# FiLM layer on one core: two slabs of 64 rows in place of four of 32, longer runs in the first store, and each projection loaded by two transfers

## The chip, the cores and the metric

The kernel runs on one core of a Trainium2 chip. Times are device microseconds of one execution; a kernel's time is the median of its runs. The profile's span, in the run that was profiled, is shorter than its time by about 1.8 us, so differences can be read in either. "Faster" or "slower" would need 2%; most of what follows is about tenths of a per cent, so the intervals are given.

## The reference

```python
batch, seq, dim, cond_dim = 32, 512, 256, 64
gamma = conditioning @ gamma_proj          # 32 x 256
beta = conditioning @ beta_proj
return (x * (1 + gamma[:, None, :]) + beta[:, None, :]).astype(np.float32)
```

x is 16.78 MB of float32 and the output is as large. The two small products need 0.14 MB: conditioning and the two projections, gamma_proj and beta_proj.

## The kernel before

x is cut into slabs. A slab puts consecutive rows of 1 KB on each of the 128 partitions, so one partition's share of a slab is one contiguous run in HBM (32 rows, 32 KB). All loads are issued on SP's queue, the constants and all stores on ACT's queue.

```python
SLABS = 4; BS = batch // SLABS; REP = P // BS; ROWS = BS * seq // P     # ROWS = 32
x_v = x.flatten_outer_dims().rearrange("(s p r) d -> s p r d", s=SLABS, p=P)
LOADS = {0: [8, 8, 8, 8], 3: [26, 6]}          # rows per load; others: one load of 32
STORES = {0: (32,), 1: (32,), 2: (32,), 3: (16, 32)}
GROUP = 16; ON_DVE = 11
# ...
nc.scalar.dma_start(out=gbproj[0::2, :], in_=gamma_proj)      # rows interleaved over
nc.scalar.dma_start(out=gbproj[1::2, :], in_=beta_proj)       # the 128 partitions
# ... conditioning is transposed and replicated by a matmul with a replicated identity;
# ... per slab a pair of matmuls gives gamma and beta, one row for each partition (PSUM);
# ... ACT copies them to SBUF (gb_s) for GpSimd; VectorE reads them from PSUM
for s in range(SLABS):
    for r0 in range(0, ROWS, GROUP):
        # VectorE: 11 of 16 rows, (gamma + 1) * x, then + beta;  GpSimd: the other 5
        # ...
        if s == 0 and r0 + GROUP == ROWS:      # "the hold": no store before the last
            nc.scalar.copy(out=held,           # but one load has landed
                           in_=slabs[-1][:, LOADS[SLABS - 1][0] - 1, 0:1])
        for e0, e1 in zip((0,) + STORES[s], STORES[s]):
            if r0 < e1 <= r0 + GROUP:
                nc.scalar.dma_start(out=o_v[s, :, e0:e1, :], in_=xs[:, e0:e1, :])
```

The hold: the copy of one element makes ACT wait for the 26-row load, so that no store begins among the loads before it, and the last 6-row load covers the time that the first store needs to get going (before: issued at 41.08, first packet at 41.96; the packets of the 6-row load end at 42.29).

Of the kernel before, what the change touches and what calls it, by code (L numbers as in the profile page):

```python
# [2 lines left out]

# [5 lines left out]


@with_exitstack
def kernel(
    ctx: ExitStack,
    tc: tile.TileContext,
    x: bass.AP,
    conditioning: bass.AP,
    gamma_proj: bass.AP,
    beta_proj: bass.AP,
    out: bass.AP,  # L20
):
    nc = tc.nc
    f32 = mybir.dt.float32
    ALU = mybir.AluOpType

    batch, seq, dim = x.shape
    cond_dim = conditioning.shape[1]
    P = 128
    SLABS = 4
    BS = batch // SLABS  # L30
    REP = P // BS
    ROWS = BS * seq // P
    assert SLABS * BS == batch and REP * BS == P and ROWS * REP == seq

    x_v = x.flatten_outer_dims().rearrange("(s p r) d -> s p r d", s=SLABS, p=P)
    o_v = out.flatten_outer_dims().rearrange("(s p r) d -> s p r d", s=SLABS, p=P)

    LOADS = {0: [8, 8, 8, 8], 3: [26, 6]}
    STORES = {0: (32,), 1: (32,), 2: (32,), 3: (16, 32)}
    GROUP = 16  # L40
    ON_DVE = 11

    consts = ctx.enter_context(tc.tile_pool(name="consts", bufs=1))
    xpool = ctx.enter_context(tc.tile_pool(name="xpool", bufs=1))
    psum = ctx.enter_context(tc.tile_pool(name="psum", bufs=1, space=bass.MemoryType.PSUM))


    cond_s = consts.tile([batch, cond_dim], f32)
    nc.scalar.dma_start(out=cond_s, in_=conditioning)  # L49

    gbproj = consts.tile([2 * cond_dim, dim], f32)
    nc.scalar.dma_start(out=gbproj[0::2, :], in_=gamma_proj)  # L52
    nc.scalar.dma_start(out=gbproj[1::2, :], in_=beta_proj)

    slabs = []
    for s in range(SLABS):
        xs = xpool.tile([P, ROWS, dim], f32, name=f"xs{s}")
        slabs.append(xs)
        r = 0
        for n in LOADS.get(s, [ROWS]):  # L60
            nc.sync.dma_start(out=xs[:, r : r + n, :], in_=x_v[s, :, r : r + n, :])
            r += n
        assert r == ROWS


    ident = consts.tile([batch, batch], f32)
    make_identity(nc, ident)
    rident = consts.tile([batch, batch * REP], f32)
    nc.vector.tensor_copy(  # L69
        out=rident.rearrange("p (b g) -> p b g", g=REP),  # L70
        in_=ident.to_broadcast([batch, batch, REP]),
    )


    cond_T = []
    for h in range(2):
        wide = consts.tile([batch, cond_dim, 2], f32, name=f"wide{h}")
        nc.vector.memset(wide, 0.0)  # L78
        nc.vector.tensor_copy(out=wide[:, :, h], in_=cond_s)  # L79
        t_p = psum.tile([2 * cond_dim, batch * REP], f32, name=f"cond_T_p{h}")  # L80
        nc.tensor.matmul(t_p, lhsT=wide.rearrange("b k h -> b (k h)"), rhs=rident,  # L81
                         start=True, stop=True)
        t_s = consts.tile([2 * cond_dim, batch * REP], f32, name=f"cond_T{h}")
        nc.vector.tensor_copy(out=t_s, in_=t_p)  # L84
        cond_T.append(t_s)

    gb_p, gb_s = [], []
    for s in range(SLABS):
        p_t = psum.tile([P, 2 * dim], f32, name=f"gb_p{s}")
        for h in range(2):  # L90
            nc.tensor.matmul(p_t[:, h * dim : (h + 1) * dim],  # L91
                             lhsT=cond_T[h][:, s * P : (s + 1) * P], rhs=gbproj,
                             start=True, stop=True)
        s_t = consts.tile([P, 2 * dim], f32, name=f"gb_s{s}")
        nc.scalar.activation(out=s_t[:, :dim], in_=p_t[:, :dim],  # L95
                             func=mybir.ActivationFunctionType.Identity,
                             bias=1.0, scale=1.0)
        nc.scalar.copy(out=s_t[:, dim:], in_=p_t[:, dim:])  # L98
        gb_p.append(p_t)
        gb_s.append(s_t)  # L100

    def rows(t, n):
        return bass.AP(tensor=t.tensor, offset=t.offset, ap=[t.ap[0], [0, n], t.ap[1]])

    held = consts.tile([P, 1], f32)
    with tc.manual_schedule():
        for s in range(SLABS):
            xs = slabs[s]
            g_p, b_p = gb_p[s][:, :dim], gb_p[s][:, dim:]
            g_s, b_s = gb_s[s][:, :dim], gb_s[s][:, dim:]  # L110
            for r0 in range(0, ROWS, GROUP):
                v = xs[:, r0 : r0 + ON_DVE, :]
                w = xs[:, r0 + ON_DVE : r0 + GROUP, :]
                nv, nw = ON_DVE, GROUP - ON_DVE
                nc.vector.scalar_tensor_tensor(out=v, in0=rows(g_p, nv), scalar=1.0, in1=v,  # L115
                                               op0=ALU.add, op1=ALU.mult)
                nc.gpsimd.tensor_tensor(out=w, in0=w, in1=rows(g_s, nw), op=ALU.mult)  # L117
                nc.vector.tensor_add(out=v, in0=v, in1=rows(b_p, nv))  # L118
                nc.gpsimd.tensor_tensor(out=w, in0=w, in1=rows(b_s, nw), op=ALU.add)  # L119
                if s == 0 and r0 + GROUP == ROWS:  # L120

                    nc.scalar.copy(out=held, in_=slabs[-1][:, LOADS[SLABS - 1][0] - 1, 0:1])  # L122

                for e0, e1 in zip((0,) + STORES[s], STORES[s]):
                    if r0 < e1 <= r0 + GROUP:
                        nc.scalar.dma_start(out=o_v[s, :, e0:e1, :], in_=xs[:, e0:e1, :])
            assert STORES[s][-1] == ROWS


# [1 line left out]
_INS = ['x', 'conditioning', 'gamma_proj', 'beta_proj']  # L131
_OUTS = [((32, 512, 256), 'float32')]


# [23 lines left out]
```

## Time and profile before

| | before |
|---|---|
| time | 84.08 us (84.04 to 84.08, 3 runs) |
| span | 82.4 us |
| DMA queues | 48.3% + 48.1% of 16 engines' span |
| VectorE, GpSimd busy | 62%, 56% |
| first packet begins, last packet ends | 1.73, 81.28 us |

The page's lines are shown in the prediction below. They are read like this: in the rows of digits each digit is a fortieth of the span, 9 meaning busy for 90% or more. A row of the table of stretches gives the stretch, then busy time (and number of instructions) of PE, weight loads, VectorE, ACT and GpSimd, then the TensorE clock, the DMA share and the GB/s moved. Bytes are credited by packet, so a stretch's GB/s wobbles with large packets, and the DMA share can pass 1.

### The profile page before, as it was taken

To read this page: it belongs to the slowest core of one execution; us is meant where nothing else is said; L and a number is where in the kernel's file an instruction comes from. 1 tells how busy PE (TensorE), PEld (TensorE's weight loads), DVE (VectorE), ACT (ScalarE), POOL (GpSimd) and SP (SyncE) were. 2 spreads that over 40 slices of the span, in tenths; PEclk is the share of its full clock that TensorE was granted. 3 is DMA by queue.
4 is the path that set the end of the run, shared out by engine and by line. 5 is a ranking of instruction groups with operands and counts; after the bars stand their busy time and mean duration, and the time that the engine had idled before them with its cause. 6 is when DMAs were issued, how large, how long until landed. Compare 5 with 4: busy or idle time off the path is not lost.

```text
span 82.4 us, 180 instructions
## 1 busy us (share of the span) xinstructions
PE 9.4 (11%) x20; PEld 5.5 (7%) x20; DVE 51.1 (62%) x23; ACT 4.1 (5%) x10; POOL 46.4 (56%) x22
## 2 busy tenths in 40 slices
PE   0069799200000000000000000000000000000000
PEld 0041478000000000000000000000000000000000
DVE  1023307999999999999999999999990000000000
ACT  0600017400000000000000000000000000000000
POOL 2000008999999999999999999999600000000000
PEclk9999999998555555555555555555555555555555
DMA  3899999979979998999797996996995999789992
GB/s 52 322 417 426 429 425 541 461 318 493 493 334 445 509 397 370 439 465 452 301 564 318 509 493 270 509 493 270 509 509 254 509 509 429 334 382 493 397 397 111
DMA packets 2080, 33.69 MB, mean 409 GB/s; under 512 B 288, under 2 KB 416, under 8 KB 544
## 3 DMA queue, kind: packets, MB, share of 16 engines
q1 hardware_dynamic: 1152, 16.78, 48.3%
q10 hardware_dynamic: 928, 16.92, 48.1%
HBM read 16.92 MB, written 16.78 MB: 409 GB/s over the span
## 4 chain that ended last, share of the span: by engine, by line
DVE 43%; issue 17%; DMA 9%; PE 4%; ACTq 1%; ACT 1%
DVE xs L115 30%; DVE xs L118 13%; DMA gbproj<-in_beta_proj_dram 9%; PE gb_p L91 4%; ACTq L52 1%; ACTq L49 0%; ACT gb_s L95 0%; ACT gb_s L98 0%
## 5 line engine op out<-in xcount | busy, mean ns | idle before, releaser
L117 POOL TENSOR_TENSOR xs<-xs,gb_s 128x1280 f32<-128x1280 f32 x8 | 23.1, 2889 | 11.5 <-ACT gb_s L95 11.5
L115 DVE SCALAR_TENSOR_TENSOR xs<-gb_p,xs 128x2816 f32<-128x2816 f32 x8 | 24.7, 3083 | 3.5 <-ACT gb_s L98 3.5
L118 DVE TENSOR_TENSOR xs<-xs,gb_p 128x2816 f32<-128x2816 f32 x8 | 24.7, 3087 | 0.3
L119 POOL TENSOR_TENSOR xs<-xs,gb_s 128x1280 f32<-128x1280 f32 x8 | 23.1, 2886 | 0.6
L91 PE MATMUL gb_p<-gbproj,cond_T 128*128 128x256 f32 x16 | 5.7, 530 | 0.6 <-DMA gbproj<-in_beta_proj_dram 0.6
L91 PEld LDWEIGHTS gb_p<-gbproj,cond_T 128*128 128x128 f32 x16 | 4.4, 280 | 3.1 <-issue 2.1
L81 PE MATMUL cond_T_p<-rident,wide 32*128 32x512 f32 x4 | 3.8, 1096 | 4.8 <-DVE rident L69 4.8
L84 DVE COPY cond_T<-cond_T_p 128x512 f32<-128x512 f32 x2 | 1.4, 692 | 3.2 <-PE cond_T_p L81 3.2
L79 DVE COPY wide<-cond_s 32x64 f32<-32x64 f32 x2 | 0.3, 182 | 3.0 <-DMA cond_s<-in_conditioning_dram 3.0
L95 ACT ACTIVATE gb_s<-gb_p 128x256 f32<-128x256 f32 x4 | 1.5, 384 | 9.3 <-PE gb_p L91 9.3
L81 PEld LDWEIGHTS cond_T_p<-rident,wide 32*128 32x128 f32 x4 | 1.2, 318 | 5.9 <-DVE rident L69 4.8
L98 ACT COPY gb_s<-gb_p 128x256 f32<-128x256 f32 x4 | 1.5, 367 | 0.0
L122 ACT COPY held<-xs 128x1 f32<-128x1 f32 x1 | 0.2, 192 | 25.3 <-DMA xs<-in_x_dram 25.3
L95 ACT ACT_TABLE_LOAD x1 | 1.3, 1283 | 2.4 <-issue 2.4
L78 DVE MEMSET wide<- 32x128 f32 x2 | 0.3, 165 | 0.8 <-PEq L142 0.8
L69 DVE COPY rident<-ident 32x512 f32<-32x512 f32 x1 | 0.4, 406 | 0.0
masks.py:197 POOL MEMSET ident<- 32x32 f32 x1 | 0.1, 114 | 0.3 <-POOLq L142 0.3
masks.py:199 POOL TENSOR_SCALAR_AFFINE_SELECT ident<-ident 32x32 f32<-32x32 f32 x1 | 0.2, 202 | 0.1
L142 POOL MEMSET const-float32-0.0<- 128x1 f32 x1 | 0.1, 104 | 0.2 <-issue 0.2
L142 POOL MEMSET const-bfloat16-1.0<- 128x1 bf16 x1 | 0.1, 107 | 0.0
L142 POOL MEMSET const-uint8-127<- 128x1 uint8 x1 | 0.1, 107 | 0.0
L142 POOL MEMSET const-float32-1.0<- 128x1 f32 x1 | 0.1, 104 | 0.0
## 6 DMA issues: line engine op xcount, KB each, us to landing
out_dram<-xs ACTq DMA_DIRECT2D x3, 4096.0 KB, 20.5
xs<-in_x_dram SPq DMA_DIRECT2D x2, 4096.0 KB, 24.6
xs<-in_x_dram SPq DMA_DIRECT2D x4, 1024.0 KB, 8.3
out_dram<-xs ACTq DMA_DIRECT2D x2, 2048.0 KB, 20.3
xs<-in_x_dram SPq DMA_DIRECT2D x1, 3328.0 KB, 35.2
xs<-in_x_dram SPq DMA_DIRECT2D x1, 768.0 KB, 35.1
gbproj<-in_gamma_proj_dram ACTq DMA_DIRECT2D x1, 64.0 KB, 6.4
gbproj<-in_beta_proj_dram ACTq DMA_DIRECT2D x1, 64.0 KB, 7.3
```

The lines of the kernel that those rows point to most:

```text
L52: nc.scalar.dma_start(out=gbproj[0::2, :], in_=gamma_proj)
L69: nc.vector.tensor_copy(out=rident.rearrange("p (b g) -> p b g", g=REP), in_=ident.to_broadcast([batch, batch, REP]),)
L81: nc.tensor.matmul(t_p, lhsT=wide.rearrange("b k h -> b (k h)"), rhs=rident, start=True, stop=True)
L84: nc.vector.tensor_copy(out=t_s, in_=t_p)
L91: nc.tensor.matmul(p_t[:, h * dim : (h + 1) * dim], lhsT=cond_T[h][:, s * P : (s + 1) * P], rhs=gbproj, start=True, stop=True)
L95: nc.scalar.activation(out=s_t[:, :dim], in_=p_t[:, :dim], func=mybir.ActivationFunctionType.Identity, bias=1.0, scale=1.0)
L98: nc.scalar.copy(out=s_t[:, dim:], in_=p_t[:, dim:])
L115: nc.vector.scalar_tensor_tensor(out=v, in0=rows(g_p, nv), scalar=1.0, in1=v, op0=ALU.add, op1=ALU.mult)
L117: nc.gpsimd.tensor_tensor(out=w, in0=w, in1=rows(g_s, nw), op=ALU.mult)
L118: nc.vector.tensor_add(out=v, in0=v, in1=rows(b_p, nv))
L119: nc.gpsimd.tensor_tensor(out=w, in0=w, in1=rows(b_s, nw), op=ALU.add)
L142: nc = _bacc.Bacc("TRN2", target_bir_lowering=False, num_devices=1)
```

## The change

The intent is fewer and larger pieces: half the slabs, so half of the small matmul and copy work in front, and the first slab's result written in runs of 64 KB. Each projection is loaded by two transfers of 32 rows.

```diff
-    SLABS = 4
+    SLABS = 2
...
-    LOADS = {0: [8, 8, 8, 8], 3: [26, 6]}
-    STORES = {0: (32,), 1: (32,), 2: (32,), 3: (16, 32)}
+    LOADS = {0: [8, 8, 8, 8, 32], 1: [32, 26, 6]}
+    STORES = {0: (64,), 1: (32, 64)}
...
-    nc.scalar.dma_start(out=gbproj[0::2, :], in_=gamma_proj)
-    nc.scalar.dma_start(out=gbproj[1::2, :], in_=beta_proj)
+    half = cond_dim // 2
+    for h, proj in enumerate((gamma_proj, beta_proj)):
+        for c0 in (0, half):
+            nc.scalar.dma_start(out=gbproj[2 * c0 + h : 2 * (c0 + half) : 2, :],
+                                in_=proj[c0 : c0 + half, :])
...
-                    nc.scalar.copy(out=held, in_=slabs[-1][:, LOADS[SLABS - 1][0] - 1, 0:1])
+                    nc.scalar.copy(out=held, in_=slabs[-1][:, ROWS - LOADS[SLABS - 1][-1] - 1, 0:1])
```

## The prediction

> **What bounds the kernel now.** I read the page from the top: the slices, then the DMA queues, then the table of stretches, and only then the chain of waits, because that chain ends at a compute instruction and would mislead here.
>
> ```profile
> span 82.4 us, 180 instructions
> PE 9.4 (11%) x20; PEld 5.5 (7%) x20; DVE 51.1 (62%) x23; ACT 4.1 (5%) x10; POOL 46.4 (56%) x22
> ...
> DVE  1023307999999999999999999999990000000000
> ...
> DMA  3899999979979998999797996996995999789992
> ...
> q1 hardware_dynamic: 1152, 16.78, 48.3%
> q10 hardware_dynamic: 928, 16.92, 48.1%
> ```
>
> The reader is to see that no compute engine is busy in the last ten of forty slices, while the DMA row is near full from the second slice to the last but one. The two DMA queues (q1 carries the loads of x, q10 the projections and the stores) take 48.3% + 48.1% = 96.4% of sixteen engines' span, or 79.4 us of 82.4. The table of stretches says where the other 3 us are:
>
> ```profile
> 0.00:1.70 1.70, 0.00 (x0) 0.00 (x0) 0.31 (x2) 0.00 (x0) 0.53 (x6) 1.00 0.00 0
> 1.70:4.00 2.30, 0.00 (x0) 0.00 (x0) 0.00 (x0) 1.28 (x1) 0.00 (x0) 1.00 0.98 310
> ...
> 12.00:40.00 28.00, 2.85 (x11) 2.05 (x9) 27.06 (x9) 2.59 (x8) 27.01 (x10) 0.64 1.00 431
> 40.00:60.00 20.00, 0.00 (x0) 0.00 (x0) 19.86 (x8) 0.19 (x1) 18.89 (x7) 0.50 1.01 430
> 60.00:80.00 20.00, 0.00 (x0) 0.00 (x0) 1.87 (x1) 0.00 (x0) 0.00 (x0) 0.50 1.01 432
> ...
> 81.30:82.40 1.10, 0.00 (x0) 0.00 (x0) 0.00 (x0) 0.00 (x0) 0.00 (x0) 0.50 0.00 0
> ```
>
> The last two columns are the DMA share and GB/s. It is 1.7 us of start, about 79.6 us at a share of 1.00, and 1.1 us of end. Loads (12 to 40) and stores (40 to 80) run at the same 430 to 432 GB/s. So the span is the sum of the packets' times on a DMA engine plus some 2.8 us that are not transfer. The trace's own list of DMA packets gives the terms; each engine gets 8 of a transfer's 128 packets, one per partition: 8 KB 309 ns (median; 326 as a mean, because the first sixteen take 366 to 1082), 16 KB 615 ns, 26 KB 992 ns, 32 KB 1221 ns as a store and 1218 as a load (means). From 16 to 32 KB a packet grows by 605 ns and from 8 to 16 by 306, so the time is nearly all bytes: 2 x 309 - 615 = 3 ns and 2 x 615.3 - 1220.6 = 10 ns are what a packet costs beyond them.
>
> The handoff matters too, for the stores are held until the 26-row load has landed:
>
> ```profile
> 38.81 2.88 POOL L119 TENSOR_TENSOR xs<-xs,gb_s 128x1280 f32<-128x1280 f32 x1
> 40.42 3.09 DVE L118 TENSOR_TENSOR xs<-xs,gb_p 128x2816 f32<-128x2816 f32 x1
> 40.86 0.19 ACT L122 COPY held<-xs 128x1 f32<-128x1 f32 x1 [25.32 <-DMA xs<-in_x_dram]
> 41.08 1.52 ACTq L126 DMA_DIRECT2D out_dram<-xs  x2
> ```
>
> The store is issued at 41.08, its first packet begins at 41.96, and the last 6-row load's packets end at 42.29: the load just covers the issue. The vector engine (its ninth and tenth instruction on x) is then at slab 2: four instructions make a slab, so slabs 0 and 1 were finished before the hold ended.
>
> [...]33.69 MB in the 79.55 us from the first packet (1.73) to the last packet's end (81.28) are 423.5 GB/s.[...] The change takes the pitch from 32 to 64 KB per partition[...]; the trace before has only the 32 KB pitch and can't test it.
>
> **The change part by part.**
> (1) *Two slabs in place of four.* The loads keep their sizes and order (8, 8, 8, 8, 32, 32, 26, 6 rows), so their packets keep their sizes; only their HBM pitch changes. 0 us.
> (2) *The stores.* Before, per engine: slabs 0 to 2 are 24 packets of 32 KB, 24 x 1220.6 = 29.29 us, and slab 3's two stores are 16 packets of 16 KB, 16 x 615.3 = 9.84 us; together 39.14 us. After: slab 0 is 8 packets of 64 KB, estimated by the slope above at 1220.6 + 2 x 605.3 = 2431 ns, 19.45 us, and slab 1 is 16 packets of 32 KB, 19.53 us; together 38.98 us. The gain is 0.16 us. If a 64 KB run is cut in two, it is 32 x 1220.6 = 39.06, a gain of 0.08.
> (3) *The projections.* The same 128 packets of 1 KB (46 ns each) in four transfers in place of two. Each transfer adds a 4-byte packet per engine of 9 ns, so +18 ns, and the five stores that become three take the same back. The two further issues cost the ACT queue about 2 x 0.5 us (its two now last 0.50 and 0.61), so the last projection is issued at about 2.8 in place of 1.7. They also go between the x packets. I estimate the landing of the last piece at 9.1 to 10.5 in place of 9.05.
> (4) *What hangs on it, off the path.* The shorter replication matrix halves the moving width of the four first matmul records (1096 ns each), saving some 2 us, but the projection matmuls wait for the last landing anyway. Only one pair of products is needed for slab 0, and the order of instructions now places it first: about four records of 0.5 us in place of six (2.91 us). So the vector engine starts at roughly 10 + 2.0 + 0.7 = 12.7, against 12.81. Its eight instructions on slab 0 are 8 x 3.06 = 24.5 us, done at 37.2, against the hold at 40.86: 3.6 us of slack, so neither an early nor a late front moves the first store. The first half of slab 1 is done at 49.5 and the second at 61.7; the DMA engines need them at 42 + 19.5 = 61.5 and at 71.3. Slack again, in both.
> (5) *Queue order.* There are sixteen transfers in both kernels and eight completion semaphores to share. With four projections the fourth load now waits for the first small transfer (landed at 4.05) and the fifth for the first load (5.64). Three loads of 1 MB are ahead of them and keep the engines busy to about 11, so no hole.
> Sum: -0.16 (2) + 0 (1, 3, 4, 5) = -0.16 us, so 84.08 - 0.16 = 83.92.
>
> **The rivals.**
> *A: the larger runs or pitch upset HBM.* Sixteen engines then write at addresses twice as far apart. For it: the trace has no 64 KB packet and no 64 KB pitch. Against it: 8, 26 and 32 KB packets, load and store, cost the same per byte. 2% of 16.78 MB of stores would be 0.8 us: 84.7.
> *B: a hole at the handoff.* The cover is 42.29 - 41.96 = 0.3 us. If the first store's issue takes longer with one more semaphore to wait on, or the first 64 KB packet starts later, sixteen engines idle for the difference. I give it up to 0.5 us: 84.4.[...]
> *C: the front is on the path after all, and its earlier or later end moves the time.* The chain of waits speaks for it, since it goes through the projections' landing and the vector instructions. Against it: that chain ends at 61.9 with the last store's issue, and that store's packets did not start until the previous one's were done. It would be worth up to 1 us either way: 83.1 to 85.1.
> *D: the larger first store takes more of the shared engines from the last small load.*[...] It moves no bytes, and the 6 rows are needed only at about 55. 0 us.
>
> **Range and chances.** The main sum is small and well measured; the runs before spread by 0.04 us. A, B and C at about one chance in ten each make the upper side somewhat longer. I predict 83.9 us, with 83.5 to 84.5 as the range of 8 in 10. A change by 2% is 1.7 us: for faster the transfers would have to outrun a rate that is flat over all sizes, 0.01; for slower A has to be strong, 0.02; within 2%, 0.97.
>
> **What would show it.** Right: 64 KB packets of about 2.43 us (or twice as many of 32 KB), a DMA share of 1.00 from 1.7 to about 81.1, stores at 430 GB/s, `held` still at about 40.9, the vector engine done with slab 0 by 38. Wrong: a store stretch under 425 GB/s with longer packets (A), a share under 1.00 around 41 to 43 (B), or a first store issued well after `held` (C).

The sum came to -0.16 us, all of it from step 2, and 84.08 - 0.16 = 83.92. The rate "flat over all sizes" is that of the trace before for packets of 8 to 32 KB: 309, 615, 992 and 1221 ns are 38.6, 38.5, 38.2 and 38.1 ns per KB; at 6 KB it is 39.7 (238 ns) and at 1 KB 46.

## The result

The changed kernel took 84.17 us (84.01 to 84.33, 6 runs) against 84.08 (84.04 to 84.35, 6 runs). The ratio of the two is 1.0005, with a 95% interval of 0.9987 to 1.0023. Ratios here are the mean time of one kernel's runs over the mean of the other's runs of the same rounds, so they are not quite the ratio of the medians quoted. The time is the same, and 84.17 lies in the predicted range.

The page after, in the lines that answer to those of before:

```profile
span 82.4 us, 153 instructions
PE 5.5 (7%) x12; PEld 3.7 (4%) x12; DVE 50.4 (61%) x23; ACT 2.8 (3%) x6; POOL 46.4 (56%) x22
...
DMA  2999999989989989999799909999956995998990
...
q1 hardware_dynamic: 1152, 16.78, 48.5%
q10 hardware_dynamic: 672, 16.92, 47.8%
```

The work of PE fell by two fifths and that of ACT by a third (9.4 to 5.5 us and 4.1 to 2.8), and 256 packets are gone from the store queue. The two DMA shares, the only lines that could move the span, went up by 0.2 and down by 0.3 points. The table of stretches, first one line of the kernel before, then the changed kernel:

```profile
4.00:12.00 8.00, 6.58 (x11) 3.46 (x12) 2.00 (x5) 0.00 (x0) 0.00 (x0) 1.00 1.01 424
```

```profile
4.00:12.00 8.00, 3.96 (x9) 2.73 (x10) 1.31 (x5) 0.99 (x1) 0.00 (x0) 1.00 1.01 402
12.00:40.00 28.00, 1.55 (x5) 0.96 (x3) 26.99 (x9) 1.29 (x4) 26.95 (x10) 0.58 1.01 432
40.00:60.00 20.00, 0.00 (x0) 0.00 (x0) 19.86 (x8) 0.19 (x1) 18.94 (x7) 0.50 1.06 458
60.00:80.00 20.00, 0.00 (x0) 0.00 (x0) 1.94 (x1) 0.00 (x0) 0.00 (x0) 0.50 0.97 416
```

From 40 to 80 us the mean is 437 GB/s (458 and 416 averaged; 64 KB packets are credited in lumps) where it was 431: the stores are no slower. The stretch from 4 to 12 us is slower: 402 GB/s at a full DMA share, where the kernel before moved 424 in the same eight microseconds. That line is the lead for the experiments. The handoff, from the timeline of the changed kernel:

```profile
40.49 3.09 DVE L121 TENSOR_TENSOR xs<-xs,gb_p 128x2816 f32<-128x2816 f32 x1
41.09 0.19 ACT L125 COPY held<-xs 128x1 f32<-128x1 f32 x1 [26.86 <-DMA xs<-in_x_dram]
41.34 0.37 ACTq L129 DMA_DIRECT2D out_dram<-xs  x1
```

The hold ends 0.23 us later than before (41.09 against 40.86) and the store follows it at once. Its first packet begins at 42.21, and the loads' last packet ends at 42.50.

### The packets, added up

The trace's list of DMA packets lets one add up what an engine has to do. This table is worked out from it (sum of a group's packet times over 16 engines, in us). The last row is from the instruction records: span's end less the landing of the last store (a transfer has 16 completion records in the trace, and its landing is the last of them).

| term | before | after | difference |
|---|---|---|---|
| all packets of the stores | 39.14 | 38.91 | -0.23 |
| excess of the 8 KB packets of x over 309 ns, after the first 48 | 0.02 | 0.38 | +0.36 |
| 1 KB packets of the projections | 0.37 | 0.39 | +0.02 |
| excess of the first 48 packets of x (start-up) | 0.54 | 0.28 | -0.25 |
| landing of the last store to the span's end | 0.83 | 0.83 | 0 |

The first 48 packets are those that begin before about 3.3 us. Their excess is from 0.28 to 0.59 over all traces (0.53 in a second trace of the changed kernel), with no relation to the kernel, so I leave that row out of the argument. The stores gave 0.23 us, a little more than predicted. Something beside the projections took 0.36 us, and that was not predicted.

### The profile page after: what moved, and what is told of

It reads as the page before. It is cut to its first block, busy times and chain, and to the rows that moved or that the text cites. A ratio compares the mean times of both kernels' runs of the same rounds, so it can differ in the third digit from the quotient of the medians.

```text
span 82.4 us, 153 instructions
## 1 busy us (share of the span) xinstructions
PE 5.5 (7%) x12; PEld 3.7 (4%) x12; DVE 50.4 (61%) x23; ACT 2.8 (3%) x6; POOL 46.4 (56%) x22
## 2 busy tenths in 40 slices
DMA packets 1824, 33.69 MB, mean 409 GB/s; under 512 B 288, under 2 KB 416, under 8 KB 544
## 4 chain that ended last, share of the span: by engine, by line
DVE 49%; issue 11%; DMA 8%; ACTq 3%; PE 2%; ACT 1%
DVE xs L118 30%; DVE xs L121 19%; DMA gbproj<-in_beta_proj_dram 8%; PE gb_p L94 2%; ACTq L55 2%; ACTq L49 0%; ACT gb_s L98 0%; ACT gb_s L101 0%
## 5 line engine op out<-in xcount | busy, mean ns | idle before, releaser
L94 PE MATMUL gb_p<-gbproj,cond_T 128*128 128x256 f32 x8 | 3.4, 607 | 3.5 <-DMA gbproj<-in_beta_proj_dram 3.5
L94 PEld LDWEIGHTS gb_p<-gbproj,cond_T 128*128 128x128 f32 x8 | 2.5, 330 | 4.8 <-issue 4.2
L84 PE MATMUL cond_T_p<-rident,wide 32*128 32x256 f32 x4 | 2.1, 670 | 4.5 <-DVE rident L72 4.5
L87 DVE COPY cond_T<-cond_T_p 128x256 f32<-128x256 f32 x2 | 0.8, 425 | 1.7 <-PE cond_T_p L84 1.7
L98 ACT ACTIVATE gb_s<-gb_p 128x256 f32<-128x256 f32 x2 | 0.8, 384 | 8.0 <-PE gb_p L94 8.0
L101 ACT COPY gb_s<-gb_p 128x256 f32<-128x256 f32 x2 | 0.7, 367 | 0.0
```

The costliest lines, as they stand in the source:

```text
L84: nc.tensor.matmul(t_p, lhsT=wide.rearrange("b k h -> b (k h)"), rhs=rident, start=True, stop=True)
L87: nc.vector.tensor_copy(out=t_s, in_=t_p)
L94: nc.tensor.matmul(p_t[:, h * dim : (h + 1) * dim], lhsT=cond_T[h][:, s * P : (s + 1) * P], rhs=gbproj, start=True, stop=True)
L98: nc.scalar.activation(out=s_t[:, :dim], in_=p_t[:, :dim], func=mybir.ActivationFunctionType.Identity, bias=1.0, scale=1.0)
L101: nc.scalar.copy(out=s_t[:, dim:], in_=p_t[:, dim:])
```

## The experiments

Twelve runs were made beside the main one, all correct (after_again repeats the changed kernel). "Excess" is the second row of the table above.

**after_again**: the changed kernel, unchanged, as a yardstick.

> The changed kernel once more, as the yardstick for the three others of this job. Theory (the span is the sum of the packets on an engine; the two traces differ by 0.05 us in the end of the last packet): within 0.1 us of the kernel before, ratio 0.998 to 1.001. Rival (the 64 KB pitch and runs upset HBM): above 1.005.

Measured: 84.22 us (84.18 to 84.38) against 84.15, ratio 1.0011 (0.9998 to 1.0023). The excess was 0.34 again, the store packets 38.91 us. The time is within the expected 0.1 us of the kernel before; the ratio lies at the upper edge of what was expected (0.998 to 1.001).

**split_only**: the kernel before, with the projections as in the changed kernel.

```diff
-    nc.scalar.dma_start(out=gbproj[0::2, :], in_=gamma_proj)
-    nc.scalar.dma_start(out=gbproj[1::2, :], in_=beta_proj)
+    half = cond_dim // 2
+    ...                       # the four transfers of the change
```

> The kernel before with its projections in two transfers each, nothing else. Theory: the last projection lands about 1 us later (near 10.0 in place of 9.05), the vector engine starts about 1 us later (13.7), and the time does not move: 84.1, ratio 0.999 to 1.001, because slab 0 is done at 26 and the stores are held to 41. Rival (the front is on the path): +0.9 us, ratio 1.01.

Measured: 84.59 us (84.53 to 84.99) against 84.15, ratio 1.0058 (1.0041 to 1.0076). That misses my expectation (0.999 to 1.001), and lies between it and the rival's. The last projection landed at 9.97 and VectorE started at 13.72, as expected. The late front is not the cause, as late_before below shows with a far later one. The packet list has two others. The excess is 0.33, as in the changed kernel. And the end is longer: 1.05 us from the last landing to the span's end in place of 0.83. SP ends the program by waiting for the eight DMA semaphores one after another, in the order of its instructions (in the trace of the kernel before from 42.73 us to 81.63). With 16 transfers the last store's semaphore comes last in that order; with 18 it comes earlier, and four more wait instructions, 0.06 us apart, follow it. SP's waits from 70 us on, before and split_only:

```profile
SPq L153 <- DMA out_dram<-xs: 19.4, 3, 9.7
```

```profile
SPq L156 <- DMA out_dram<-xs: 48.6, 1, 48.6
```

In the kernel before, one wait after another ends as a store lands; in split_only SP stands 48.6 us at one wait, for the last store, and has the others still to pass. The excess (+0.31) and the end (+0.22), with -0.06 from the store packets, make +0.47; the ratio says 0.49.

**slabs_only**: the two slabs and the stores, without the split projections (the changed kernel with the two original lines).

> The two slabs and their stores without the split projections. Theory: the store packets sum to 38.91 us an engine in place of 39.14, so 0.1 to 0.25 us faster than before (83.85 to 84.0), the projections land near 9.1, and the vector engine starts about 1 us earlier than in the changed kernel (11.9) without any effect on the end. Rival: faster than the changed kernel by the same 0.9 us by which the front is earlier.

Measured: 84.14 us (84.01 to 84.20) against 84.15, ratio 0.9996 (0.9982 to 1.0009). The store packets add up to 38.90 us and the excess is 0.02. VectorE started at 11.89, 0.98 us earlier than in the changed kernel, and nothing came of it. With 14 transfers the end is 0.95 us, so of the 0.24 us that the stores give, 0.12 goes there. The 0.1 us that is left is inside the interval. My expectation of 0.1 to 0.25 overlooked the end and was missed: the ratio gives 0.03. From the table of stretches, first before, then slabs_only, then split_only:

```profile
4.00:11.00 7.00, 5.58 (x8) 2.67 (x9) 2.00 (x5) 0.00 (x0) 0.00 (x0) 1.00 1.02 425
```

```profile
4.00:11.00 7.00, 3.94 (x9) 2.71 (x10) 1.33 (x5) 0.00 (x0) 0.00 (x0) 1.00 1.02 428
```

```profile
4.00:11.00 7.00, 4.67 (x6) 1.99 (x7) 2.00 (x5) 0.96 (x1) 0.00 (x0) 1.00 1.02 405
```

The share of busy DMA time is the same in all three; the bytes moved are not. With the split, and with either number of slabs, 20 GB/s or more are missing for 7 us. That is 0.14 MB or more, which at 424 GB/s is 0.33 us.

**split_alt**: the split by alternate rows in place of halves. In the changed kernel the rows 0 to 31 of a projection go to partitions 0 to 63, and the rows 32 to 63 to the other half. Here each of the four transfers spreads over all partitions.

```diff
-        for c0 in (0, half):
-            nc.scalar.dma_start(out=gbproj[2 * c0 + h : 2 * (c0 + half) : 2, :],
-                                in_=proj[c0 : c0 + half, :])
+        for c0 in (0, 1):
+            nc.scalar.dma_start(out=gbproj[2 * c0 + h :: 4, :], in_=proj[c0::2, :])
```

> The changed kernel with each projection split by alternate rows in place of halves: four transfers of 32 rows as before, but each spreads over all 128 partitions, where the changed kernel's lie in one half of them. Theory (in the changed kernel the 8 KB packets of x that run beside the projections are longer, 0.31 to 0.38 us an engine, because each small transfer goes to one half of the partitions[...]): the excess falls to about 0.02 us, as with unsplit projections, the last packet ends about 0.3 us earlier and the time is 83.8 to 84.0, ratio to before 0.995 to 0.998. Rival (four transfers of 32 rows cost it, wherever they land): the excess stays at 0.3 and the time at 84.2.

Measured: 84.01 us (83.92 to 84.12) against 84.14, ratio 0.9983 (0.9970 to 0.9996). The excess fell to 0.01. The number of transfers was not the cause. The time fell a little less than I had put (the ratio's range was 0.995 to 0.998). This is the one kernel whose interval lies below 1: it beats the kernel before by 0.17%. It was not run in the same rounds as the changed kernel; by the ratios (1.0005 and 1.0011) it beats that one by 0.2 to 0.3%. The changed kernel and split_alt from 4 to 11 us:

```profile
4.00:11.00 7.00, 2.96 (x6) 1.99 (x7) 1.31 (x5) 0.99 (x1) 0.00 (x0) 1.00 1.01 399
```

```profile
4.00:11.00 7.00, 3.32 (x7) 2.25 (x8) 1.33 (x5) 0.99 (x1) 0.00 (x0) 1.00 1.02 426
```

**halves**: the cross-check. slabs_only, two transfers, but gamma in partitions 0 to 63 and beta in 64 to 127.

```diff
-    nc.scalar.dma_start(out=gbproj[0::2, :], in_=gamma_proj)
-    nc.scalar.dma_start(out=gbproj[1::2, :], in_=beta_proj)
+    nc.scalar.dma_start(out=gbproj[:cond_dim, :], in_=gamma_proj)
+    nc.scalar.dma_start(out=gbproj[cond_dim:, :], in_=beta_proj)
...                           # wide is [batch, 2, cond_dim] to match
```

> The two slabs with unsplit projections, but gamma's 64 rows in partitions 0 to 63 and beta's in 64 to 127 in place of interleaved (the other matmul operand is reordered to match, so the result is the same). Theory (one half of the partitions at a time): the excess of the 8 KB packets, 0.02 us with interleaved rows, comes back at 0.2 to 0.4 us, and the time is 84.3 to 84.6 where the interleaved one had 84.14. Rival (the number of transfers counts): excess 0.02, time 84.1.

Measured: 84.57 us (84.37 to 84.63) against 84.14, ratio 1.0044 (1.0032 to 1.0056). The excess came back at 0.37 with only two transfers. Together with split_alt this settles what matters: whether a small transfer spreads over all partitions or lies in one half of them.

```profile
4.00:11.00 7.00, 3.62 (x8) 2.47 (x9) 1.33 (x5) 0.00 (x0) 0.00 (x0) 1.00 1.02 405
```

**runs32**: the first slab stored in two transfers of 32 KB runs.

```diff
-    STORES = {0: (64,), 1: (32, 64)}
+    STORES = {0: (32, 64), 1: (32, 64)}
```

> The changed kernel with the first slab stored in two transfers of 32 KB runs. Theory: 16 packets of 1218 ns in place of 8 of 2427 ns an engine, 19.49 against 19.42, so +0.07 us against the changed kernel, below what five rounds resolve. Rival (a large packet starts late or is slow): 0.2 to 0.5 us faster than the changed kernel.

Measured: 84.86 us (84.68 to 85.05) against 84.15, ratio 1.0081 (1.0064 to 1.0098). This does not test what I meant: neither the theory nor the rival was tried. The hold stands ahead of the slab's last store only, so the first half went out when its rows were done: its first packet begins at 29.1 us, among the loads. The packets of 32 KB loads grew from a mean of 1218 to 1246 ns (up to 1851), +0.45 us an engine, while the later loads gained 0.08. The growth is not spread over the loads: it is in 16 packets, as many as there are engines, that began between 28.6 and 30.3 us, just before or as the stores set in (1441 to 1851 ns). The 32 packets of 32 KB loads that began after 30.4 us took 1213 ns beside the stores, no more than before. So what this run shows is a price paid once where stores begin among loads. Against runs32_held below it comes to 0.3 us (ratios 1.0081 and 1.0046).

**runs32_held**: the same with both stores behind the hold.

```diff
-                if s == 0 and r0 + GROUP == ROWS:
+                if s == 0 and r0 + GROUP == STORES[0][0]:
```

> The changed kernel with the first slab stored in two transfers of 32 KB runs, this time with both behind the hold (in the earlier trial of this the first went out at 29 us, beside the loads). Theory: 19.49 in place of 19.42 us of packets an engine, +0.07; seventeen transfers, so the last store's semaphore is the first of eight that the end waits for, three waits of 0.06 us more at the end, about +0.17; together 84.4 to 84.5 where the changed kernel has 84.2. Rival (64 KB packets cost or save much more than their bytes): over 0.3 us away from the changed kernel on either side beyond that.

Measured: 84.53 us (84.40 to 84.74) against 84.14, ratio 1.0046 (1.0034 to 1.0058). The store packets add up to 39.04 us, 0.13 more than with 64 KB runs, and the end is 0.99 us, 0.16 more. Expected was +0.24 in sum, and the distance of the two medians is 0.31 to 0.36. So the 64 KB runs save about a tenth of a microsecond against two of 32 KB.

**rows1k**: the other end of the scale, the first slab stored as even and odd rows, so in runs of 1 KB.

```diff
+                        if s == 0:
+                            for k in range(2):
+                                nc.scalar.dma_start(out=o_v[s, :, e0 + k : e1 : 2, :],
+                                                    in_=xs[:, e0 + k : e1 : 2, :])
```

> The changed kernel with the first slab stored as its even and its odd rows, two transfers whose runs are 1 KB in place of one of 64 KB runs; the bytes are the same. Theory (a packet costs its bytes at 37 ns per KB and a fixed 3 to 10 ns more, so only many small packets are felt): 512 packets an engine of 46 ns, as the 1 KB rows of the projections take, are 23.6 us in place of 8 of 2427 ns, 19.42 us, so +4.1 us, and +0.17 for the end of seventeen transfers: 88.5 (88 to 89.2). Rival (the time of a store depends on its bytes alone): 84.4. Second rival (the supply of so many packets or the writes to HBM limit it): over 90.

Measured: 89.63 us (89.52 to 89.82) against 84.16. The direction held, but the time is above my range. The 1 KB store packets took 48.7 ns, not 46, so 512 of them are 1.4 us longer than I had counted: 24.95 us in place of 19.42 is +5.5, and 5.4 was measured against the changed kernel. That these agree is partly chance: the end (+0.16) and a longer hole before the first store (0.55 us an engine in place of 0.18) come on top, while the 1 KB packets overlap one another, which takes 0.8 us off the sum of their times. At 37.8 ns per KB (the step from 16 to 32 KB packets) a 1 KB store packet takes 11 ns more than its bytes, about what a large packet does too. In the table of stretches of this kernel, 1 KB runs in the first line, 32 KB runs in the last:

```profile
44.00:60.00 16.00, 0.00 (x0) 0.00 (x0) 15.90 (x6) 0.00 (x0) 15.04 (x6) 1.00 1.04 347
...
66.00:86.00 20.00, 0.00 (x0) 0.00 (x0) 0.00 (x0) 0.00 (x0) 0.00 (x0) 1.00 1.03 436
```

The DMA share is full in both lines. Only the GB/s tell them apart.

**late_before and late_after**: the projections moved onto the load queue behind the first 48 rows' worth of loads, 6 MB of x. (The text below garbles this amount; the code is what ran.)

```diff
-    LOADS = {0: [8, 8, 8, 8], 3: [26, 6]}                   # late_before
+    LOADS = {0: [8, 8, 8, 8], 1: [16, 16], 3: [26, 6]}
+            if (s, r) == (1, 16):     # both projections on nc.sync here
...
-    LOADS = {0: [8, 8, 8, 8, 32], 1: [32, 26, 6]}           # late_after
+    LOADS = {0: [8, 8, 8, 8, 16, 16], 1: [32, 26, 6]}
+            if (s, r) == (0, 48):     # the four transfers on nc.sync here
```

> The kernel before with its projections queued behind 5 MB... that is, behind slab 0 and half of slab 1 on the load queue (16 MB of x in all), so that they land near 18.5 in place of 9.05 and the vector engine starts about 8 us later, near 21. Theory: with four slabs slab 0 is done near 33.5 and slab 1 near 46, both ahead of the hold (40.9) and of their turn (51.7), and the last slab near 70, ahead of 76: no change, 84.1 to 84.4. Rival (the chain of waits is right that the front is on the path): +8 us.

> The changed kernel with the same delay: projections behind the first 48 rows of slab 0, landing near 18.5 in place of 9.97. Theory: slab 0 is now one store of 64 rows, done near 37.3 + 8.3 = 45.7, 4.4 us after the hold, so the DMA engines idle from 42.5 to about 46.6 and the time is about 88.2 (87.5 to 89). If the change took no slack away, it would stay at 84.1.

Measured: late_before 84.33 us (84.27 to 84.40) against 84.18, ratio 1.0014 (0.9997 to 1.0031), though VectorE started at 21.19 in place of 12.81. late_after 89.69 us (89.25 to 89.79), ratio 1.0640. In late_after the store waits for VectorE and not for the hold:

```profile
40.79 0.19 ACT L126 COPY held<-xs 128x1 f32<-128x1 f32 x1 [17.60 <-DMA xs<-in_x_dram]
...
43.09 3.09 DVE L122 TENSOR_TENSOR xs<-xs,gb_p 128x2816 f32<-128x2816 f32 x1
...
46.26 0.36 ACTq L130 DMA_DIRECT2D out_dram<-xs  x1
```

```profile
42.00:47.00 5.00, 0.00 (x0) 0.00 (x0) 4.97 (x3) 0.00 (x0) 5.00 (x2) 0.50 0.00 0
```

The same five microseconds of late_before:

```profile
42.00:47.00 5.00, 0.00 (x0) 0.00 (x0) 4.96 (x3) 0.00 (x0) 5.00 (x2) 0.50 1.09 468
```

The changed kernel's DMA engines stand still from 42.2 to 47.1. The same delay of about 8 us is free with four slabs and costs 5.5 us with two. That is more than I expected (4.0, at most 4.8). The profiled run, 89.25 us, is accounted for: slab 0 was done at 46.18 rather than 45.7, so the engines stood still for 4.9 us, and seventeen transfers make the end 0.16 longer. It was the fastest of the four, and what the other three spent their 0.4 to 0.5 us more on I did not find.

**cover1 and cover10**: the last two loads cut at 31 and 1 rows, or at 22 and 10, in place of 26 and 6.

> The changed kernel with its last two loads cut at 31 and 1 rows in place of 26 and 6, so the load that covers the issue of the first store is 8 packets of 46 ns (0.37 us an engine) in place of 8 of 238 (1.91 us). Theory: from the end of the guarding load's packets (40.6) to the first store packet (42.2) are 1.6 us, so the engines idle for 1.2 to 1.6 us and the time is 85.3 to 85.8. Rival (the stores catch up later, or the end is set by the vector engine): no change, 84.1.

> The same two loads cut at 22 and 10 rows: 8 packets of about 385 ns, 3.1 us of cover. Theory: the small hole at 41.9 to 42.3 (5 to 13 of 16 engines active in the changed kernel's trace, about 0.1 us an engine) closes: 0.05 to 0.15 us faster than the changed kernel, near 84.0. Rival: the hole is not there, no difference or +0.1.

Measured: cover1 85.77 us (85.64 to 85.86) against 84.18, ratio 1.0183 (1.0166 to 1.0201). The engines' mean idle time from 38 to 48 us is 1.52 us in its packet list, where the changed kernel has 0.18 (0.11 in its second trace). The hold now ends later:

```profile
42.55 0.19 ACT L125 COPY held<-xs 128x1 f32<-128x1 f32 x1 [28.15 <-DMA xs<-in_x_dram]
42.79 0.36 ACTq L129 DMA_DIRECT2D out_dram<-xs  x1
```

cover10 took 84.37 us (84.15 to 84.43) against 84.18, ratio 1.0010 (0.9992 to 1.0027), like the changed kernel. The hole is closed in its packet list, and its store packets are 0.15 us an engine shorter, yet nothing is gained. The engines are not in step: the 16 parts of the last load land over about 0.65 us in either kernel. In the changed kernel the hole levels them, and the 16 parts of the last store land within 0.21 us. With cover10 they still lie 0.66 us apart. So what the hole takes is the lead of the engines that are ahead; the slowest engine, which sets the end, never waited there. That is a reading of the landings, and no run was made to test it. (The second trace of the changed kernel has 0.49 us and 0.17.)

### The whole account

For each kernel the changes against the before kernel in the store packets, the excess and the end are added up (us, from the traces) and set beside the measured difference (ratio less 1, times 84.15). runs32 has its loads' +0.37 added.

| kernel | stores | excess | end | sum | measured |
|---|---|---|---|---|---|
| after (two traces) | -0.23 | +0.36, +0.32 | 0 | +0.13, +0.09 | +0.04, +0.09 |
| split_only | -0.06 | +0.31 | +0.22 | +0.47 | +0.49 |
| slabs_only | -0.24 | 0.00 | +0.12 | -0.12 | -0.03 |
| split_alt | -0.22 | -0.01 | 0 | -0.22 | -0.14 |
| halves | -0.22 | +0.35 | +0.12 | +0.25 | +0.37 |
| runs32_held | -0.10 | +0.31 | +0.16 | +0.37 | +0.39 |
| runs32 | -0.21 | +0.29 | +0.16 | +0.61 | +0.68 |
| late_before | -0.06 | -0.01 | +0.15 | +0.08 | +0.12 |
| cover10 | -0.38 | +0.32 | 0 | -0.06 | +0.08 |

No row is off by more than 0.14 us, which is about the half-width of the intervals (0.10 to 0.15 us); the worst is cover10, whose shorter store packets brought nothing. The three terms fit ten traces of nine kernels as well as the noise lets one tell. cover1, late_after and rows1k are left out: their 1.5 to 5.5 us come from idle engines and from 1 KB packets, as told above.

## Why the prediction was right

The verdict, within 2%, and the range held, for the reason given: the DMA engines are full from the first packet to the last, and the bytes do not change. (From the first packet to the last, the kernel before moved 33.69 MB in 79.55 us, 423.5 GB/s, at a DMA share of about 1.00. That no higher rate is to be had was the author's estimate; no run tried for one.) The sign did not hold: -0.16 us was predicted, and the measured +0.04 has an interval of -0.11 to +0.19. That 84.17 is nevertheless inside the range is in part luck: the range was made long upwards for rivals A, B and C, none of which came true, and another term, missing from the sum, used that room.

Step 1 (the loads keep their sizes, 0 us) held, and with it the estimate that a pitch of 64 KB in place of 32 costs nothing: slabs_only has the new pitch, its excess is 0.02 us, as before, and its 32 KB loads take 1218 ns, as before.

Step 2 (the stores) held. A 64 KB packet takes 2427 ns, estimated was 2431. The gain was 0.23 us where 0.16 was put; part of it is that the 32 KB packets took 1218 in place of 1221 ns.

Step 3 (the projections) is the one that failed. The landing was right (9.97, in 9.1 to 10.5). The cost was put at +18 ns an engine, from counting the packets of the four transfers alone. It was 0.33 to 0.38 us, nearly all of it excess: the packets of x beside a transfer that lies in one half of the partitions grew, which split_alt (excess 0.01) and halves (0.37) show. I had counted the transfers and not looked at the partitions they go to. This term is larger than the gain of step 2 and turned the predicted -0.16 into the measured +0.04 to +0.09. split_alt, without that excess, has the predicted change: -0.14.

Step 4 (the front is off the path) held: the first four matmul records took 2.07 us together in place of 3.77 (a saving of some 2 us was put), VectorE started at 12.87 (12.7 was put) and finished slab 0 at 37.45. late_before and late_after show the slack itself, and also that the change spent most of it: slab 0 used to be done at 25.1, with the hold at 40.9; now 3.6 us remain. The profile before could not show this as a cost, and in the time it is none.

Step 5 (no hole from the shared semaphores) held: the fourth and fifth loads waited as put (issued at 3.89 and 5.48), and the DMA share is 1.01 from 4 to 12 us. I had not seen that the number of transfers also sets where the last store's semaphore stands in the final waits. Before and after have sixteen, so it cost nothing here.

Rival A (large runs or pitch upset HBM) fell: the stores are faster (their packets take 38.91 us in place of 39.14). Rival B (a hole at the handoff) was there in one trace of the changed kernel, 0.18 us an engine, but the second trace has 0.11, as before has, and slabs_only and split_alt, with the same 64 KB store, have 0.04 and 0.02; closing it gained nothing. cover1 shows that a real one, 1.5 us, is paid in full. Rival C (the front) fell by late_before. Rival D cost nothing. The rule of turns that it assumed is not shown; what the list of the kernel before shows is that the packets of two queues mix: the 128 packets of 1 KB of the projections begin from 5.11 to 8.23 us, and 145 packets of 8 KB of x begin in the same time. But the small load's last packet ended at 42.50 against 42.29, and the end did not follow it.

Why a transfer into one half of the partitions lengthens the packets of x is not shown. The size is that of the small packets themselves: 128 packets of 46 ns are 5.9 us, over 16 engines 0.37 us, which is the excess. It is as if every small packet were paid twice. But this does not say why the interleaved transfer pays only 0.01 to 0.02 us. Nor is it enough to say that a small packet holds up the packets of x for the same half of the partitions: a count in the trace of halves speaks against it in this simple form. The trace names no partitions, but about half of the packets of x should then be as before, yet all 111 of the 8 KB packets that begin between 6.2 and 8.8 us are longer (mean 348 ns, none under 318). Of these, 46 begin after gamma's transfer has landed at 7.75, when only beta's, into the other half, is under way. The cause behind the excess stays open.

## What to carry to other kernels

When the DMA share is full from end to end, a change that only regroups the same bytes into larger runs can win what the packets cost beyond their bytes, here some 0.2 us, and that is to be worked out before anything is built. A small transfer beside a large one is better spread over all partitions (excess 0.01 to 0.02 us here, in place of 0.29 to 0.38), and the check is the GB/s, not the busy share, in the microseconds where they overlap (from 4 to 11 us 399 to 405 against 425 to 428, at a share of 1.01 to 1.02 in all). Larger units of work use up slack that no profile charges for: the same delay was free before the change and cost 5.5 us after it.

## What the runs measured beside the question

- A small transfer into one half of the partitions lengthened the packets of other transfers: 8 KB packets beside it took a mean of 345 to 350 ns in place of 309 in the worst microsecond (after, after_again, split_only, halves), 0.3 to 0.4 us an engine in all for 128 KB. Interleaved rows cost 0.01 to 0.02 us.
- A store in runs of 1 KB took 48.7 ns a packet and ran at 347 GB/s, where 32 KB runs in the same kernel (rows1k) ran at 436; 8.39 MB in such runs cost 5.4 us. The part beyond the bytes was some 11 ns at 1 KB and 10 ns or less from 8 KB on.
- SP's final waits took 0.06 us each, in an order fixed by the program, so 14, 16, 17 and 18 transfers over eight semaphores ended 0.95, 0.83, 0.99 and 1.05 us after the last landing.
- Where stores began among loads (runs32), 16 packets of 32 KB loads, as many as there are engines, took 1441 to 1851 ns in place of 1218, 0.46 us an engine, and the loads after them took no longer than without stores (32 KB 1213 ns, 26 KB 987).
